# FoX output projection by block products, with GpSimd making the weight sums and two of the seven products beside the last pass of attention

## The chip, the cores and the metric

The kernel runs on one core of a Trainium2 chip. A core has TensorE (PE: matmuls, with its weight loads in a row of their own, PEld), VectorE (DVE), ScalarE (ACT), GpSimd (POOL) and SyncE (SP), which here issues all DMAs. The metric is the time of one execution on the device in microseconds (us), as the median of several runs.

## The reference

Two layers on 1024 tokens of width 1024, float32. Each layer has a token mixer (forgetting attention in layer 0, gated linear attention, GLA, in layer 1) and a SwiGLU part of hidden width 2816, both normed before, modulated by a conditioning vector and added back with a gate. The change touches the last product of the first mixer, `o @ w_out`, a 1024 x 1024 by 1024 x 1024 product whose result is gated and added to `x`.

```python
def forgetting_attention(h, w_in, b_f, w_out):
    ...
    for blk in range(S // Q_BLOCK):
        ...
        p = jax.nn.softmax(logits, axis=-1).astype(v.dtype)
        outs.append(jnp.einsum('bhqk,bkhd->bqhd', p, v[:, :qe]))
    o = jnp.concatenate(outs, axis=1).reshape(B, S, D_MODEL)
    return o @ w_out

def reference(...):
    ...
        x = x + g1[:, None, :] * y
        h = modulate(rms_norm(x, norm2_g[i]), sh2, sc2)
        x = x + g2[:, None, :] * swiglu(h, ffn_w_in[i], ffn_w_out[i])
    return rms_norm(x, final_g)
```

## The kernel before

**Layout.** Activations lie transposed: feature tiles of 128 partitions by 1024 tokens, eight of them, each in two token halves of 512. A product of float32 matrices is made of three matmuls in TensorE's rounded format: each operand is split into a high part (a cast on ScalarE) and a low part (a subtraction on VectorE or GpSimd), and `mm3` (L304) adds high times high, high times low and low times high into one PSUM bank. `split` (L173) does this for activations. `load_w` (L220) does it for weights: a DMA into one of the three raw buffers `wr`, two casts on ScalarE, and the low part in four quarters, three on GpSimd and one on VectorE, into a pair of buffers of the ring `ws`. `Weights` (L290) holds the list of all weight loads in program order and keeps up to `depth` of them issued ahead.

**Order.** All engines run their own instructions in order. The order on each engine is chosen when the program is built, by a scheduler that follows the program order and moves ready work ahead. `weave` (L130) interleaves two generators by their stated costs.

**Attention.** Eight passes of two heads, p = 0 to 7. `attention(p)` (L1356) takes, for each head, four groups of 256 queries in the order 0, 3, 1, 2 (L1344). `scores` makes logits on TensorE, a minimum on VectorE (L1287), the exponential on ScalarE (L1291), a reciprocal on VectorE (L1292) and the scaling on GpSimd (L1293). `outputs` transposes the probabilities on TensorE, splits them and multiplies with v; the result goes to a tile `oT` (L1342). One group's outputs are made behind the next group's scores. After passes 0 to 6 the tile is stored to `oT_d` (L1354); that of pass 7 stays on the chip. In the loop at L1384 each pass is woven with the q, k and v projections of the next one (`qk_proj`, L1246, and `v_half`). Until pass 7 small steps of the conditioning (`ada0`, raw rows also in `wr`) run beside.

**The FoX output projection.** `fox_tail` (L1459) is woven with pass 7 (L1474). It reloads o tiles 0 to 3 from `oT_d`, splits them into `oh`, and `out_chunk` (L1412) multiplies k tiles 0 to 3 with the weights for eight output tiles and two token halves, adding each result with the gate to `xs` on VectorE (L1431). Behind it, in `ffn` (L1494), `last_chunk` (L1436) does k tiles 4 to 7, first token half 0, then token half 1, and sums the squares (`SumSq`, L759) for the norm. The norm of half 0 (L1543, with L1533 and L1541) runs while TensorE does half 1; the feed-forward matmuls begin right behind, `plain_tile` (L1669), with the norm of half 1 inside them. The weights come in by `out_loads` (L882, L1062): four loads for k tiles 0 to 3, and four for k tiles 4 to 7, twice.

**Layer 1** already makes its output projection by block products (`out_blocks`, L2392, and `out_ends`, L2467), with weight sums made ahead on GpSimd (`ow_sums`, L985), and hands them to `ffn` by its argument `blocks`.

Of the kernel before, what the change touches and what calls it, by code (L numbers as in the profile page):

```python
# [9 lines left out]
F32 = mybir.dt.float32  # L10
# [6 lines left out]
P = 128  # L17
# [36 lines left out]
def trunk(ctx, tc, x, c, ada_w, ada_b, norm1_g, norm2_g, ffn_w_in, ffn_w_out,  # L54
# [972 lines left out]

    OW_G = (0, 1, 2)

    def ffn_loads(l):  # L1030

        blk = lambda gr, ab, *after: (op_block, l, gr, ab, *after)
# [24 lines left out]
    for p in range(7):  # L1057
# [200 lines left out]

    oTs = {}

    def scores(u):

# [189 lines left out]


    idle = [s_ for s_ in list(vring.q)[:4] + list(qk_free)[:3]]
    oh = new_h("oh")
    x_slots = idle + [list(otr.q)[-1]]
    xs = [big.tile([P, S], F32, tag=x_slots[k], name=f"x0_{k}") for k in range(8)]

    def fox_tail():  # L1459
        for k in range(4):  # L1460
            reload_h(oT_d, oh, k, "or")

        nc.sync.dma_start(xs[0], xT_d[0])

        def ahead(k):
            if 3 <= k < 6:
                reload_h(oT_d, oh, k + 1, "or")
            if k < 7:
                nc.sync.dma_start(xs[k + 1], xT_d[k + 1])
            yield 0.01  # L1470
# [1078 lines left out]
```

## Time and profile before

| what | value |
|---|---|
| median of 3 runs | 2354.34 us (2350.84 to 2356.11) |
| the profiled execution | 2352.71 us, its span 2351.0 us |
| granted TensorE clock, mean | 0.996 |
| share of the span: PE, DVE, ACT, POOL | 99%, 76%, 48%, 48% |
| DMA moved | 383.38 MB, mean 163 GB/s |

A row of the timeline gives the start, the duration, the engine, the line, the operation, the tiles (written <- read) and the shapes; a bracket gives idle time of the engine ahead of it and what ended it. A row of groups gives the count, the busy time, the mean duration in ns of one, and the idle time ahead. A row of stretches gives the length and then, for each engine, busy time and the count of instructions, at the end the granted clock, the share of the DMA engines and the GB/s. The times of one view are those of one execution. Buffer numbers are left out of names; `fo0470p_b` is the bank for k tiles from 4, output tile 7, of the first run over token half 0.

### The profile page before, as it was taken

To read this page: it belongs to the slowest core of one execution; us is meant where nothing else is said; L and a number is where in the kernel's file an instruction comes from. 1 tells how busy PE (TensorE), PEld (TensorE's weight loads), DVE (VectorE), ACT (ScalarE), POOL (GpSimd) and SP (SyncE) were. 2 spreads that over 40 slices of the span, in tenths; PEclk is the share of its full clock that TensorE was granted. 3 is DMA by queue.
4 is the path that set the end of the run, shared out by engine and by line. 5 is a ranking of instruction groups with operands and counts; after the bars stand their busy time and mean duration, and the time that the engine had idled before them with its cause. 6 is when DMAs were issued, how large, how long until landed. Compare 5 with 4: busy or idle time off the path is not lost. (4 is left out here: it accounts for less than half of the span.)

```text
span 2351.0 us, 35555 instructions
## 1 busy us (share of the span) xinstructions
PE 2327.1 (99%) x12168; PEld 1981.4 (84%) x12168; DVE 1780.7 (76%) x2947; ACT 1121.9 (48%) x2166; POOL 1139.3 (48%) x1005
## 2 busy tenths in 40 slices
PE   8999999999999999999999999999999999999999
PEld 7888888888888888888888898898888888888888
DVE  6578787886688888886787665568787777876887
ACT  6666566665453333344334644345544333345236
POOL 1334444533355656664563431335456666664651
PEclk8999999999999999999999999999999999999999
DMA  8423343332435545458774443455434544458674
GB/s 263 149 85 109 104 122 95 122 126 99 129 101 178 188 157 172 156 180 305 261 255 156 143 127 90 140 179 170 140 111 158 176 149 159 139 189 299 238 262 142
DMA packets 349614, 383.38 MB, mean 163 GB/s; under 512 B 25372, under 2 KB 286648, under 8 KB 349432
## 3 DMA queue, kind: packets, MB, share of 16 engines
q1 hardware_dynamic: 349432, 381.11, 49.3%
q8 instruction: 96, 1.57, 0.3%
q14 instruction: 86, 0.70, 0.1%
HBM read 279.76 MB, written 101.25 MB: 162 GB/s over the span
## 5 line engine op out<-in xcount | busy, mean ns | idle before, releaser
L174 ACT CAST o_s<-xv_s 128x512 fp32r<-128x512 f32 (+1 forms) x392 | 236.4, 610 | 340.2 <-PE p_b L307 257.2
L175 DVE TENSOR_TENSOR o_s<-xv_s,o_s 128x512 fp32r<-128x512 f32 (+1 forms) x392 | 336.5, 863 | 43.7 <-ACT o_s L174 43.0
L307 PE MATMUL p_b<-B,o_s 128*128 128x512 f32 x608 | 236.0, 389 | 0.0
L306 PE MATMUL p_b<-B,o_s 128*128 128x512 f32 x608 | 235.9, 389 | 0.0
L305 PE MATMUL p_b<-B,o_s 128*128 128x512 f32 x608 | 235.4, 390 | 0.0
L1293 POOL TENSOR_SCALAR lp_s<-lp_s,st 128x128 f32<-128x128 f32 (+7 forms) x128 | 96.9, 761 | 247.9 <-DVE st L1292 229.0
L940 POOL TENSOR_TENSOR ex_s<-xv_s,xv_s 128x512 f32<-128x512 f32 (+1 forms) x64 | 94.8, 1481 | 239.8 <-DMA xv_s<-in_ffn_w_in_dram 121.9
L305 PE MATMUL p_b<-T,o_s 128*128 128x512 f32 x480 | 186.8, 389 | 0.0
L306 PE MATMUL p_b<-T,o_s 128*128 128x512 f32 x480 | 186.7, 389 | 0.0
L307 PE MATMUL p_b<-T,o_s 128*128 128x512 f32 x480 | 181.2, 389 | 0.0
L307 PEld LDWEIGHTS p_b<-B,o_s 128*128 128x128 f32 x608 | 114.1, 188 | 23.9
L305 PEld LDWEIGHTS p_b<-B,o_s 128*128 128x128 f32 x608 | 114.1, 188 | 23.7 <-DVE x L1659 0.2
L306 PEld LDWEIGHTS p_b<-B,o_s 128*128 128x128 f32 x608 | 114.1, 188 | 23.5
L1291 ACT ACTIVATE lp_s<-lp_s,st 128x128 f32<-128x128 f32 (+7 forms) x128 | 99.3, 776 | 57.9 <-DVE st L1287 56.5
L942 POOL TENSOR_TENSOR xv_s<-ex_s,xv_s 128x512 f32<-128x512 f32 (+1 forms) x64 | 93.8, 1466 | 60.6 <-DVE o_s L175 57.7
L1659 DVE TENSOR_TENSOR ex_s<-ex_s,p_b 128x512 f32<-128x512 f32 x140 | 94.2, 681 | 38.0 <-PE p_b L307 37.8
L174 ACT CAST pt_s<-t_b 128x512 fp32r<-128x512 f32 (+1 forms) x160 | 79.7, 547 | 73.5 <-PE t_b L1313 72.9
L952 POOL TENSOR_TENSOR xv_s<-xv_s,xv_s 128x512 f32<-128x512 f32 x48 | 65.5, 1364 | 92.3 <-issue 50.4
L175 DVE TENSOR_TENSOR pt_s<-t_b,pt_s 128x512 fp32r<-128x512 f32 (+1 forms) x160 | 96.2, 630 | 15.9 <-ACT pt_s L174 15.4
L246 POOL TENSOR_TENSOR w_l_s<-w__s,w_h_s 128x256 fp32r<-128x256 f32 x90 | 69.4, 800 | 77.1 <-ACT w_h_s L242 59.2
L307 PEld LDWEIGHTS p_b<-T,o_s 128*128 128x128 f32 x480 | 90.1, 188 | 18.7
L306 PEld LDWEIGHTS p_b<-T,o_s 128*128 128x128 f32 x480 | 90.1, 188 | 18.7
(1527 smaller groups left out, 7409.5 us busy)
## 6 DMA issues: line engine op xcount, KB each, us to landing
xv_s<-in_ffn_w_in_dram SPq DMA_DIRECT2D x176, 256.0 KB, 3.3
hid_B<-x SPq DMA_DIRECT2D x66, 512.0 KB, 2.8
ad_s<-in_ada_w_dram SPq DMA_DIRECT2D x384, 64.0 KB, 2.4
hid_T<-x SPq DMA_DIRECT2D x44, 512.0 KB, 2.9
xv_s<-in_ffn_w_out_dram SPq DMA_DIRECT2D x88, 256.0 KB, 3.5
ada_s<-in_ada_w_dram SPq DMA_DIRECT2D x96, 128.0 KB, 2.8
T2o<-hid_T SPq DMA_DIRECT2D x22, 512.0 KB, 7.5
T1o<-hid_T SPq DMA_DIRECT2D x22, 512.0 KB, 6.2
```

What stands on the lines that cost most here:

```text
L174: nc.scalar.copy(hi, src)
L175: nc.vector.tensor_sub(lo, src, hi.bitcast(F32))
L246: (nc.gpsimd if i < 3 else nc.vector).tensor_sub(lo[:, cs], rw[:, cs], hi[:, cs].bitcast(F32))
L305: nc.tensor.matmul(ps, ah, bh, start=start, stop=False, skip_group_check=chain)
L306: nc.tensor.matmul(ps, ah, bl, start=False, stop=False, skip_group_check=chain)
L307: nc.tensor.matmul(ps, al, bh, start=False, stop=stop, skip_group_check=chain)
L940: nc.gpsimd.tensor_add(s1, a21, a22)
L942: nc.gpsimd.tensor_sub(a11, s1, a11)
L952: nc.gpsimd.tensor_sub(r[A12], r[A12], r[A11])
L1291: nc.scalar.activation(lp, lp, AF.Exp, bias=mcur, scale=-1.0, accum_out=st[:, qi, 2:3])
L1293: nc.gpsimd.tensor_scalar(lp, lp, st[:, qi, 3:4], 1.0, op0=ALU.mult, op1=ALU.mult)
L1659: nc.vector.tensor_add(d, d if src is None else dest(G, src), ps)
```

## The change

The projection is made by the seven products of the Winograd form of Strassen's algorithm, one level deep: the 8 output tiles are taken as four pairs g, the k tiles and the tokens are halved. With a = o tiles 0 to 3 and c = o tiles 4 to 7, and the index for the token half, the activation blocks are B11 = a1, T1 = a0 - a1, T2 = c0 - T1, T3 = c0 - a0, B22 = c0, B21 = c1, T4 = c1 - T2. On the weight side A11, A12 and A22 are blocks of the weights, and four sums (called 5, 6, 3 and 7) are made by `fox_sums`: eight steps in passes 2 to 5 load a part of the weights, make the sums with four GpSimd operations each and store them in DRAM (`fw_d`). `fox_loads` reads 14 weight loads of the old size: blocks or sums.

Beside pass 7, `fox_tail` now makes B11 and T1 (two pairs g at a time, two banks), and the splits of T2 and B22 for the three o tiles that are stored. Behind it come `fox_blocks` (T2, B22, T3) and, as the end with the norm beside it, `fox_ends` (B21 and T4, output tile by output tile), both called from `ffn` by its argument `blocks`. The differences of activations are on GpSimd but for one. a and c are reloaded for T3, B21 and T4 into slots that attention used. Results are still added to `xs` on VectorE, 40 times in place of 32.

```diff
+    fw_d = {(nm_, g): tc.dram_tile([HALF, P], F32, name=f"fw{nm_}{g}") for nm_ in (5, 6, 7, 3) for g in range(4)}
+    def fox_src(g, ab):
+        return fox_w_out[0][psl(4 * ab[1], 4), psl(2 * g + ab[0])]
+    def fox_sums():
+        for g in range(4):
+            for s_ in (0, 2):
+                t = wr([P, 2, 2, 2 * P], F32, f"fw{g}{s_}")
+                for h in range(2):
+                    nc.sync.dma_start(t[:, h], fox_w_out[0][psl(4 * h + s_, 2), psl(2 * g, 2)]
+                                      .rearrange("(k p) m -> p k m", p=P))
+                (a11, a21), (a12, a22) = ((t[:, h, :, 0:P], t[:, h, :, P:2 * P]) for h in range(2))
+                nc.gpsimd.tensor_add(a22, a21, a22)
+                nc.gpsimd.tensor_sub(a21, a11, a21)
+                nc.gpsimd.tensor_sub(a11, a22, a11)
+                nc.gpsimd.tensor_sub(a12, a12, a11)
+                for nm_, a in ((5, a22), (7, a21), (6, a11), (3, a12)):
+                    nc.sync.dma_start(fw_d[(nm_, g)].rearrange("(k p) m -> p k m", p=P)[:, s_:s_ + 2], a)
+                yield
+    def fox_loads():
+        two = lambda a, b, nm_: (load_w, (a, b), nm_)
+        r = [two(fox_src(g, A11), fw_d[(5, g)], f"fa{g}") for g in range(4)]
+        r += [two(fw_d[(nm_, g)], fw_d[(nm_, g + 1)], f"f{nm_}{g}") for nm_ in (6, 3, 7) for g in (0, 2)]
+        return r + [two(fox_src(g, A12), fox_src(g, A22), f"fe{g}") for g in range(4)]
...
-    loads += out_loads(fox_w_out[0], 0, 4) + 2 * out_loads(fox_w_out[0], 4, 4)
+    loads += fox_loads()
...
+        if 1 < p < 6:
+            next(fw_sums)
...
+    fw_sums = fox_sums()
...
+    F_SL = {"B11": 0, "T3": 0, "T1": 4, "B21": 4, "T2": 8, "T4": 8, "B22": 12}
+    fa3 = big.tile([P, S], F32, tag=acc_sl[0], name="fa3")
+    def fb_split(nm_, k, y, lo_=nc.vector):
+        t = fb[nm_][k] = big.tile([P, 2, HALF], FR, tag=H_SL[F_SL[nm_] + k], name=f"fb{nm_}{k}")
+        nc.scalar.copy(t[:, 0], y)
+        lo_.tensor_sub(t[:, 1], y, t[:, 0].bitcast(F32))
+    def fox_raw(k, t=None):
+        t = wr([P, S], F32, f"or{k}") if t is None else t
+        nc.sync.dma_start(t, oT_d[k])
+        return t
+    def fox_prod(ps, w, c, t, ks, start):
+        for k in ks:
+            mm3(ps, w.hi[:, k, psl(c)], w.lo[:, k, psl(c)], t[k][:, 0], t[k][:, 1], start and k == ks[0],
+                k == ks[-1], True)
+            yield 0.65
+    def fox_add(m, hf, ps):
+        nc.vector.scalar_tensor_tensor(xs[m][:, hsl(hf)], ps, mcol(0, 2, m), xs[m][:, hsl(hf)],
+                                       op0=ALU.mult, op1=ALU.add)
     def fox_tail():
-        for k in range(4):
-            reload_h(oT_d, oh, k, "or")
...
-        yield from out_chunk(0, 4, oh, xs, 0, 2, "fo", (0, 1), before=ahead)
-    weave(attention(7), 27.0, fox_tail(), 36.0, LAGS)
-    split(oh[7].hi, oh[7].lo, oTs[7])
+        for k in ALL:
+            a = fox_raw(k, fa3 if k == 3 else None)
+            fb_split("B11", k, a[:, h1_])
+            if k < 3:
+                nc.gpsimd.tensor_sub(a[:, h0_], a[:, h0_], a[:, h1_])
+                fb_split("T1", k, a[:, h0_])
+            else:
+                nc.gpsimd.tensor_sub(a[:, h1_], a[:, h0_], a[:, h1_])
+                fb_split("T1", k, a[:, h1_])
+        for m in (0, 1):
+            nc.sync.dma_start(xs[m], xT_d[m])
+        feed.depth = 2
+        for g in (0, 2):
+            ws_, ps_ = [], []
+            for i in range(2):
+                ws_.append(feed.next())
+                ps_.append(pj([P, HALF], F32, f"fo{g + i}p"))
+                yield from fox_prod(ps_[i], ws_[i], 0, fb["B11"], ALL, True)
+                for m in (2 * (g + i), 2 * (g + i) + 1):
+                    fox_add(m, 1, ps_[i])
...
+            for i in range(2):
+                k = g + i
+                if k < 3:
+                    c, a = fox_raw(4 + k), fox_raw(k)
+                    nc.gpsimd.tensor_sub(a[:, h1_], a[:, h1_], a[:, h0_])
+                    nc.gpsimd.tensor_add(a[:, h1_], c[:, h0_], a[:, h1_])
+                    fb_split("T2", k, a[:, h1_])
+                    fb_split("B22", k, c[:, h0_])
+                yield from fox_prod(ps_[i], ws_[i], 1, fb["T1"], ALL, False)
+                for m in (2 * (g + i), 2 * (g + i) + 1):
+                    fox_add(m, 0, ps_[i])
+    weave(attention(7), 27.0, fox_tail(), 21.0, LAGS)
+    def fox_blocks(views):
+        feed.depth = 3
+        c3, pa, w6 = oTs[7], [bank(i, [P, HALF], f"fp{i}") for i in (0, 1, 6, 7)], []
+        for g in ALL:
+            if g % 2 == 0:
+                w6.append(feed.next())
+            run(fox_prod(pa[g], w6[-1], g % 2, fb["T2"], range(3), True))
+        nc.vector.tensor_sub(fa3[:, h1_], c3[:, h0_], fa3[:, h1_])
+        fb_split("T2", 3, fa3[:, h1_])
+        fb_split("B22", 3, c3[:, h0_])
+        for g in ALL:
+            run(fox_prod(pa[g], w6[g // 2], g % 2, fb["T2"], (3,), False))
+            fox_add(2 * g, 0, pa[g])
+        ac = []
+        for k in range(3):
+            a, c = (big.tile([P, S], F32, tag=slots["b"][2 * k + i], name=f"fr{k}{i}") for i in range(2))
+            fox_raw(k, a)
+            fox_raw(4 + k, c)
+            ac.append((a, c))
+        ac.append((fa3, c3))
+        for a, c in ac:
+            nc.gpsimd.tensor_sub(a[:, h0_], c[:, h0_], a[:, h0_])
+        for k, (a, c) in enumerate(ac):
+            fb_split("T3", k, a[:, h0_])
+        sv = views()
+        sq = SumSq(sv, 0, LATE1)
+        for g in ALL:
+            pb = bank(2 + g, [P, HALF], f"fq{g}")
...
+            run(fox_prod(pb, w, g % 2, fb["B22"], ALL, True))
+            fox_add(2 * g, 0, pb)
+            sq(g, xs[2 * g][:, h0_])
+        for k, (a, c) in enumerate(ac):
+            if k < 3:
+                nc.gpsimd.tensor_add(a[:, h1_], a[:, h0_], a[:, h1_])
+            fb_split("B21", k, c[:, h1_])
+            nc.gpsimd.tensor_sub(c[:, h1_], c[:, h1_], a[:, h1_])
+        for g in ALL:
...
+            run(fox_prod(pa[g], w, g % 2, fb["T3"], ALL, False))
+            fox_add(2 * g + 1, 0, pa[g])
+            sq(4 + g, xs[2 * g + 1][:, h0_])
+            fox_add(2 * g + 1, 1, pa[g])
+            fb_split("T4", g, ac[g][1][:, h1_])
+        return sq, sv
+    def fox_ends(sv, behind):
+        sq = SumSq(sv, 1, LATE1, False)
+        for m in range(8):
...
+            ps = bank((2, 3, 4, 5, 0, 1, 4, 5)[m], [P, HALF], f"fe{m}")
...
+                run(fox_prod(ps, w, m % 2, fb["T4" if m % 2 else "B21"], ALL, True))
+            fox_add(m, 1, ps)
+            sq(m, xs[m][:, h1_])
+        return sq
...
-    ffn(0, oh, xs, slots, "fo", lambda: mid(0, 1), norm_mixer)
+    ffn(0, None, xs, slots, "fo", lambda: mid(0, 1), norm_mixer, None, (fox_blocks, fox_ends))
```

More of the change, by code (lines that the diff above doesn't have):

```diff
@@ L1474, in trunk @@
-    weave(attention(7), 27.0, fox_tail(), 36.0, LAGS)
-    split(oh[7].hi, oh[7].lo, oTs[7])
+    h0_, h1_ = hsl(0), hsl(1)
+    ALL = range(4)
+    F_SL = {"B11": 0, "T3": 0, "T1": 4, "B21": 4, "T2": 8, "T4": 8, "B22": 12}
+    fb = {nm_: [None] * 4 for nm_ in F_SL}
+    fa3 = big.tile([P, S], F32, tag=acc_sl[0], name="fa3")
[3 more added lines that the diff above has]
+        lo_.tensor_sub(t[:, 1], y, t[:, 0].bitcast(F32))
@@ new lines, in trunk @@
+    weave(attention(7), 27.0, fox_tail(), 21.0, LAGS)
[27 more added lines that the diff above has]
+            pb = bank(2 + g, [P, HALF], f"fq{g}")
+            if g % 2 == 0:
+                w = feed.next()
+            run(fox_prod(pb, w, g % 2, fb["B22"], ALL, True))
[7 more added lines that the diff above has]
+        for g in ALL:
+            if g % 2 == 0:
+                w = feed.next()
+            run(fox_prod(pa[g], w, g % 2, fb["T3"], ALL, False))
[4 more added lines that the diff above has]
+        return sq, sv
@@ new lines, in fox_ends @@
+    def fox_ends(sv, behind):
+        sq = SumSq(sv, 1, LATE1, False)
+        for m in range(8):
+            if m % 2 == 0:
+                w = feed.next()
+            ps = bank((2, 3, 4, 5, 0, 1, 4, 5)[m], [P, HALF], f"fe{m}")
+            with ExitStack() as es:
+                for m_, ins in behind:
+                    if m >= m_:
+                        es.enter_context(tc.issue_after(ins))
+                run(fox_prod(ps, w, m % 2, fb["T4" if m % 2 else "B21"], ALL, True))
+            fox_add(m, 1, ps)
+            sq(m, xs[m][:, h1_])
+        return sq
```

12 lines of the change are left out of this document (4 added, 8 removed).

## Prediction

> **What bounds the kernel now.** I read the page first, its span and first part, then the table of stretches (windows) around the place of the change, then single rows of the timeline.
>
> ```profile
> span 2351.0 us, 35555 instructions
> ## 1 busy us (share of the span) xinstructions
> PE 2327.1 (99%) x12168; PEld 1981.4 (84%) x12168; DVE 1780.7 (76%) x2947; ACT 1121.9 (48%) x2166; POOL 1139.3 (48%) x1005
> ```
>
> PE is busy 99% of the span. A busy PE is not yet a PE at its peak, since a 512-column matmul is drawn 0.39 us long and a gap can hide in that, so the spacing of starts decides. These are the last matmuls of the projection and the first of the feed-forward part:
>
> ```profile
> 639.75 0.39 PE L305 MATMUL fo1471p_b<-ohh,wo_768h_s 128*128 128x512 f32 x1
> ...
> 642.24 0.39 PE L307 MATMUL fo1471p_b<-ohh,wo_768l_s 128*128 128x512 f32 x1
> 642.47 0.39 PE L305 MATMUL p_b<-B,o_s 128*128 128x512 f32 x1
> ```
>
> Twelve starts in 2.72 us: one matmul costs 0.2267 us, and the projection hands over without a gap. Now the stretches: passes 2 to 5 of attention (where the weight sums will go), pass 6, pass 7, the rest of the projection, a busy piece of the feed-forward part, and the last 54 us of the GLA output projection, which already works by block products.
>
> ```profile
> core 0: us, PE busy (x) PEld busy (x) DVE busy (x) ACT busy (x) POOL busy (x), PEclk, DMA share, GB/s
> 190.00:442.00 252.00, 249.63 (x1658) 221.52 (x1658) 198.86 (x496) 154.27 (x333) 126.42 (x184) 1.00 0.36 111
> 472.60:531.20 58.60, 56.41 (x340) 47.27 (x339) 47.10 (x118) 40.03 (x82) 19.50 (x28) 1.00 0.39 128
> 531.20:604.00 72.80, 72.71 (x425) 62.05 (x424) 45.73 (x117) 35.51 (x79) 24.40 (x32) 1.00 0.24 85
> 604.00:642.40 38.40, 38.40 (x178) 31.76 (x177) 29.61 (x43) 21.48 (x36) 16.91 (x17) 1.00 0.51 165
> 660.00:700.00 40.00, 40.00 (x178) 33.14 (x177) 39.78 (x58) 21.54 (x37) 17.21 (x7) 1.00 0.28 86
> 1643.00:1697.00 54.00, 54.00 (x247) 44.95 (x246) 41.33 (x57) 27.49 (x46) 27.96 (x20) 1.00 0.40 127
> ```
>
> The clock is 1.00 throughout. Pass 7 loses 0.09 us of PE time in 72.8, since the projection's first 192 matmuls fill the waits of attention; pass 6, with half as many fillers (96 matmuls of the last q and k projections), loses 2.19 us in 58.6. The rest of the projection loses nothing. So every matmul taken out here is worth its 0.2267 us as long as the other engines keep up, and VectorE, at 63% and 77% in the third and fourth row, is the one to watch.
>
> **The change, part by part.** *Matmuls.* Before: 8 column tiles, 2 token halves, 8 k tiles, 3 matmuls each, 384. After: 7 products of 4 column pairs, 4 k tiles, 3 matmuls, 336. Gone: 48 x 0.2267 = **-10.9 us**. Beside pass 7 stand 96 instead of 192, behind it 240 instead of 192. So pass 7 shrinks by up to 96 x 0.2267 = 21.8 us, to 51, and the part behind it grows by 10.9, to 54.4 us.
>
> *Thinner cover of pass 7.* Its fillers then have the density of pass 6. At that row's idle share (2.19 / 58.6) a stretch of 51 us loses 1.9 us. VectorE's work in it hardly shrinks: where three oh splits fall away, six half-width splits of T2 and B22 come, and the 16 adds stay:
>
> ```profile
> L175 DVE TENSOR_TENSOR ohl<-or_s,ohh x7: 1204/1226/1627, 503.9 to 550.5; 128x1024 fp32r<-128x1024 f32 x7
> ```
>
> So about 46 of 51 us, 90%, with score reductions queued behind splits. I take **+3 us**, one more than the row, as gaps also hide in the drawn length. Bounds: 0 (nothing lost, as in pass 7 now) and 6, three times the row's share.
>
> *Weight sums.* Eight steps, each two loads of 256 KB, four GpSimd operations on 256 elements and four stores of 128 KB, in passes 2 to 5. The nearest row:
>
> ```profile
> L468 POOL TENSOR_TENSOR acc_s<-acc_s 128x256 f32<-128x256 f32 x26 | 19.2, 740 | 1.2
> ```
>
> 32 x 0.74 = 23.7 us on a GpSimd that is half idle there (126.4 of 252). What hides it is PE's own work, 249.6 of 252. Queued behind it on GpSimd are the softmax scalings (L1293), on SyncE the weight and ada loads, when a store waits for GpSimd; each step also takes one turn of the three raw buffers (wr), which weights and ada rows share:
>
> ```profile
> engine line waited for: us in total, times, longest us
> DVE acc_s L505 <- DMA ada_s<-in_ada_w_dram: 8.4, 5, 2.1
> ```
>
> PE lost 2.37 us there with 126 us of GpSimd work; in proportion 23.7 us more cost **+0.5 us**, my value. Bounds 0 and 5: eight such waits of 2.1 us, of which PE feels at most 2.37 / 8.4.
>
> *Behind pass 7.* VectorE gets 28 splits of 512 columns for 8 of 1024, 40 adds for 32, and a quarter of 14 weight loads for 12; ScalarE the matching casts (it is half idle). GpSimd gets 11 differences of 512 columns here (and 10 beside pass 7). Some of those run one after the other with VectorE, as these two answers (VectorE, then GpSimd) show:
>
> ```profile
> 1645.64 1.78 DVE L175 TENSOR_TENSOR goB<-gs_s,goB 128x512 fp32r<-128x512 f32 x1
> ...
> 1648.66 0.68 DVE L175 TENSOR_TENSOR goT<-og_s,goT 128x512 fp32r<-128x512 f32 x1
> ```
>
> ```profile
> 1645.12 1.74 POOL L1025 TENSOR_TENSOR ow_s<-xv_s,ow_s 128x512 fp32r<-128x512 f32 x1
> 1647.49 1.30 POOL L2450 TENSOR_TENSOR gs_s<-gs_s,og_s 128x512 f32<-128x512 f32 x1 [0.63 <-DVE goB L175]
> ```
>
> The same split takes 0.68 us alone and 1.78 when a GpSimd operation has begun 0.52 us ahead of it; it ends 0.56 us after that one. GpSimd takes 1.30 alone. So I add up the two engines' SBUF work as if they shared one door. Durations of the other kinds:
>
> ```profile
> 538.06 0.41 DVE L246 TENSOR_TENSOR wo_768l_s<-wo_s,wo_768h_s 128x256 fp32r<-128x256 f32 x1
> ...
> 589.21 0.48 DVE L1287 CUSTOM_DVE_ANT_0 lp_s<-s_b,cum_s,st 128x256 f32<-128x256 f32 x1
> ...
> 603.54 0.42 DVE L1342 TENSOR_TENSOR oT_s<-o_b,ot 64x256 f32<-64x256 f32 x1 [0.86 <-ACT ot L1341]
> ...
> 621.71 0.73 DVE L1431 SCALAR_TENSOR_TENSOR x<-fo0470p_b,modc,x 128x512 f32<-128x512 f32 x1
> ...
> 631.91 5.35 DVE L1533 SCALAR_TENSOR_TENSOR ya_s<-x,amul,rb_b 128x512 f32<-128x512 f32 x8
> ...
> 638.38 0.75 DVE L1541 SCALAR_TENSOR_TENSOR B<-ya_s,modc,B 128x512 fp32r<-128x512 f32 x1
> ```
>
> ```profile
> 557.57 2.32 POOL L246 TENSOR_TENSOR wo_0l_s<-wo_s,wo_0h_s 128x256 fp32r<-128x256 f32 x3 [1.61 <-ACT wo_0h_s L242]
> ...
> 591.59 0.90 POOL L1293 TENSOR_SCALAR lp_s<-lp_s,st 128x768 f32<-128x768 f32 x1 [4.78 <-DVE st L1292]
> 595.12 2.31 POOL L246 TENSOR_TENSOR wo_512l_s<-wo_s,wo_512h_s 128x256 fp32r<-128x256 f32 x3 [2.63 <-ACT wo_512h_s L242]
> 601.66 2.31 POOL L246 TENSOR_TENSOR wo_256l_s<-wo_s,wo_256h_s 128x256 fp32r<-128x256 f32 x3 [4.23 <-ACT wo_256h_s L242]
> 612.03 2.14 POOL L246 TENSOR_TENSOR wo_768l_s<-wo_s,wo_768h_s 128x256 fp32r<-128x256 f32 x3 [8.06 <-ACT wo_768h_s L242]
> ...
> 629.47 1.02 POOL L715 TENSOR_TENSOR rs<-rs,mhalf 128x4 f32<-128x4 f32 x1
> ```
>
> GpSimd: 11 x 1.30 + 10 loads x 2.32 + 4 sums of squares x 1.30 + the root, 1.0 = 43.7 us. VectorE with both inputs in SBUF: 14 splits and one difference x 0.68 + 10 x 0.41 + 6 sums of squares x 0.68 + five norm splits x 0.75 + four feed-forward weights x 0.68 = 24.9 us. Together 68.6 us for a part of 54.4: 14.2 too many if nothing is done ahead. But the slots of T3's raw tiles are free when the last scores are reduced (589.7), 14 us before the last attention output (603.5), and in the 20 us from 592 to 612 GpSimd works under 6. The 9 differences of the six reloaded tiles (11.7 us), three T3 splits (2.0) and the first two loads (5.5) fit there: 19.2 us against 14.2. It fits, with little to spare. On VectorE alone the 24 adds (24 x 0.73 = 17.5) and eight norm products (5.35) on top make about 48 us of 54.4, between the fourth row of the table (77%) and the GLA row (77%) and the 99% of 660 to 700, where PE still loses nothing. The narrow place is the end: before, the last add of token half 0 started at 621.7, the first norm split at 638.4, and PE took it up at 642.5, 4.1 us later; now four T4 splits (2.7 us) and the weights' share for the end products (1.6) stand ahead of the norm in VectorE's queue. I take **+2 us**. Bounds: 0, as the GLA row has it (PE 54.0 of 54), and 14.2, if nothing gets ahead.
>
> The Trainium skill, page "SBUF — State Buffer", section "SBUF: two separate sides", speaks against the change here: it says that GpSimd and a VectorE operation with two SBUF inputs hold a shared pair of ports by turns, for a whole instruction, and the later one blocks. The trace agrees (1.78 for 0.68). By a plain overlap of the two engines this part would cost 0, by that rule anything up to the 14.2 above.
>
> *Transfers.* Behind pass 7 come six reloads (3 MB) and two weight loads more (1 MB): the row's 165 GB/s x 38.4 us = 6.3 MB become 10.5 MB in 54.4 us, 193 GB/s. The page's slices show more than that elsewhere:
>
> ```profile
> GB/s 263 149 85 109 104 122 95 122 126 99 129 101 178 188 157 172 156 180 305 261 255 156 143 127 90 140 179 170 140 111 158 176 149 159 139 189 299 238 262 142
> ```
>
> So nothing is added; the bound is +1 us.
>
> *Sum*: -10.9 + 3 + 0.5 + 2 = **-5.4 us**. The profiled execution took 2352.7 us, 1.7 around its span of 2351.0, so it would take 2347.3. The median of the three runs, 2354.3, lies 1.6 higher; from there I forecast **2348.9 us**. About 0.2%, 4.7 us, is what a measurement of this kernel can tell from no change.
>
> **The rivals.** *All of it is kept.* Nothing but the sums costs anything: -10.4, 2343.9 us. For it: GLA, same products, PE 54.0 of 54. Against it: there no softmax chain runs beside them.
>
> *The last pass is bound by VectorE.* Pass 7 loses the 6 us of its bound, and the 4.3 us of splits that stand ahead of the norm delay the feed-forward part in full: -10.9 + 6 + 0.5 + 4.3 = -0.1, 2354.2 us. For it: 90% of VectorE in 51 us, and pass 6 losing 2.19 at 80%. Against it: the weights and the casts run ahead on other engines. This is also the case in which the change does what it says and nothing comes of it.
>
> *Slower: GpSimd and VectorE by turns.* T3's reloads land after pass 7, the 11 differences stand behind weight splits in GpSimd's queue, VectorE's splits wait for them, and PE waits for T3 and T4: the 14.2 us come in full, -10.9 + 3 + 0.5 + 14.2 = +6.8, 2361.1 us. It decides from the point where more than 7.4 us of the 14.2 fail to get ahead (10.9 - 3 - 0.5). For it: 68.6 us for 54.4, and the reloads are issued late in the program. Against it: GpSimd's idle 14 us ahead, and SyncE free to load there. The shared ports of the page named above are this mechanism.
>
> **How the numbers follow.** Forecast (-2.5 to -8) 0.46; all kept 0.16; bound by VectorE 0.24; slower by turns 0.14. Of the forecast two thirds (0.31) lie beyond 4.7 us: faster 0.16 + 0.31 = 0.47. Slower by over 4.7 us: most of the last case, 0.13, and 0.02 of the third: 0.15. The rest, 0.38, is within 0.2%. The range goes from 2342.5 (all kept, less the spread of the runs) to 2358.5, half-way into the slower case; some 0.1 lies above and 0.08 below. The forecast's own range is 2346 to 2352.
>
> **What would show it.** Right: 336 matmuls of the projection at 0.227; pass 7 shorter by 18 to 20 us with 2 to 4 us of PE idle in it; GpSimd's T3 differences before the last attention output; the first feed-forward matmul within 2 us of the last one of the projection; passes 2 to 5 as long as before within 1 us. Wrong: T3 or T4 matmuls waiting for a split behind GpSimd (slower case); score reductions late behind T1, T2 and B22 splits (third case); waits for ada or weight loads in passes 2 to 5, or a gap where the second token half of the feed-forward part begins.

## The result, and the profile after

The changed kernel took 2379.22 us (median of four runs, 2376.09 to 2380.26), the kernel before 2354.82 beside it. The ratio is 1.0107, with a 95% interval from 1.0095 to 1.0119. It is slower by about 25 us; forecast were 5 us less, and the range up to 2358.5 did not hold the time.

The head of the page of the changed kernel:

```profile
span 2377.6 us, 35758 instructions
## 1 busy us (share of the span) xinstructions
PE 2331.4 (98%) x12120; PEld 1983.5 (83%) x12120; DVE 1795.3 (76%) x2978; ACT 1132.1 (48%) x2190; POOL 1200.3 (50%) x1064
```

There are 48 matmuls fewer, as the change says, and the span is 26.6 us longer. To see where, I cut both traces at the last output matmul of each pass and at the first matmul of the feed-forward part. These are the stretches of the kernel before: passes 1 to 4 (this is where the weight sums are made; the prediction called these passes 2 to 5), pass 5, pass 6, pass 7, and the rest up to the feed-forward part.

```profile
core 0: us, PE busy (x) PEld busy (x) DVE busy (x) ACT busy (x) POOL busy (x), PEclk, DMA share, GB/s
172.80:423.50 250.70, 248.33 (x1650) 220.14 (x1649) 197.10 (x499) 152.11 (x328) 123.33 (x179) 1.00 0.36 109
423.50:484.70 61.20, 59.96 (x393) 52.61 (x391) 48.01 (x123) 37.07 (x79) 28.98 (x42) 1.00 0.38 124
484.70:540.90 56.20, 54.48 (x331) 45.93 (x331) 46.09 (x113) 39.36 (x82) 20.73 (x29) 1.00 0.42 143
540.90:602.80 61.90, 61.90 (x361) 52.89 (x360) 38.06 (x95) 29.17 (x62) 18.11 (x24) 1.00 0.19 66
602.80:642.50 39.70, 39.70 (x185) 32.84 (x184) 30.12 (x44) 21.86 (x37) 18.07 (x19) 1.00 0.50 160
```

And the same five in the changed kernel:

```profile
core 0: us, PE busy (x) PEld busy (x) DVE busy (x) ACT busy (x) POOL busy (x), PEclk, DMA share, GB/s
175.10:434.50 259.40, 252.05 (x1647) 222.55 (x1646) 196.32 (x496) 152.40 (x328) 141.76 (x207) 0.99 0.44 133
434.50:495.70 61.20, 59.59 (x393) 52.57 (x392) 48.48 (x125) 37.04 (x79) 31.29 (x44) 1.00 0.40 123
495.70:554.50 58.80, 53.28 (x317) 44.70 (x315) 45.35 (x119) 39.54 (x87) 27.83 (x32) 0.97 0.46 150
554.50:618.90 64.40, 54.68 (x304) 45.24 (x302) 52.32 (x107) 35.20 (x76) 39.97 (x40) 0.92 0.41 131
618.90:668.90 50.00, 45.31 (x210) 37.47 (x209) 40.98 (x63) 25.66 (x45) 22.97 (x24) 0.99 0.48 155
```

The projection's matmuls stand 58, 161 and 165 in the last three stretches before, and 42, 104 and 190 after (counted in the two traces; the scheduler also drew 50 matmuls of T2 and B22 forward into pass 7). At 0.2267 us each, pass 6 should have become 3.6 us shorter and the rest after pass 7 5.7 us longer. So the stretches lost:

| stretch | length | matmuls moved | lost |
|---|---|---|---|
| up to the end of pass 0 | +2.3 | 0 | 2.3 |
| passes 1 to 4 | +8.7 | 0 | 8.7 |
| pass 5 | 0.0 | 0 | 0.0 |
| pass 6 | +2.6 | -3.6 | 6.2 |
| pass 7 | +2.5 | -12.9 | 15.4 |
| rest of the projection | +10.3 | +5.7 | 4.6 |
| feed-forward part to the end | +0.2 | 0 | 0.2 |

The column adds up to 37.4, and 37.4 - 10.9 = 26.5 us, which is the difference of the spans (26.6) but for rounding. Pass 0 is the same work in all kernels here but two, and took between 172.7 and 176.5 us in their fourteen traces, so its 2.3 us are scatter. The 0.2 us of the last row is a balance of two losses: the changed kernel loses 2.9 us behind the handover to a slow clock (last section), and the kernel before has a pause and a slow clock of its own in that part (2.21 us at 1500.5 and a granted clock of 0.50 in the 3.4 us from 1500.8). Three places are left.

**The end of pass 7.** VectorE there, then TensorE, from the timeline of the changed kernel:

```profile
603.60 1.75 DVE L1498 TENSOR_TENSOR fbT<-fr,fbT 128x512 fp32r<-128x512 f32 x1 [2.98 <-POOL fr L1575]
605.27 1.75 DVE L1498 TENSOR_TENSOR fbB<-fr,fbB 128x512 fp32r<-128x512 f32 x1
606.95 1.74 DVE L1498 TENSOR_TENSOR fbT<-fr,fbT 128x512 fp32r<-128x512 f32 x1
608.72 0.42 DVE L1374 TENSOR_TENSOR oT_s<-o_b,ot 64x256 f32<-64x256 f32 x1
```

```profile
603.89 1.39 PE L1345 MATMUL t_b<-ident,lp_s 128*128 128x128 f32 x11
609.29 0.36 PE L1359 MATMUL o_b<-pt_s,v_s 128*128 128x256 f32 x1 [4.01 <-DVE oT_s L1374]
612.51 1.22 PE L1359 MATMUL o_b<-pt_s,v_s 128*128 128x256 f32 x4 [2.87 <-DVE pt_s L175]
```

Three splits of T3 and B21, raw tiles `fr`, stand on VectorE ahead of an attention output (L1374); the first of them waits 2.98 us for GpSimd. The first T3 product starts at 625.0 and the first B21 product at 640.4, 20 us later and more, but TensorE waits 4.01 us for that output and then 2.87 us for splits of probabilities. The windows of 4 us show what follows:

```profile
604.00:608.00 4.00, 1.28 (x12) 1.04 (x10) 4.00 (x3) 2.89 (x7) 4.00 (x3) 1.00 0.02 4
608.00:612.00 4.00, 0.36 (x1) 0.19 (x1) 3.94 (x6) 0.73 (x2) 4.00 (x5) 0.74 0.00 0
612.00:616.00 4.00, 3.49 (x10) 3.00 (x11) 4.00 (x5) 1.75 (x3) 3.92 (x3) 0.50 0.44 131
616.00:620.00 4.00, 4.00 (x21) 3.35 (x20) 2.00 (x4) 0.74 (x2) 0.00 (x0) 0.91 0.00 0
```

VectorE and GpSimd are both busy all the time while TensorE stands, and when its work comes back, the granted clock is 0.50 for four microseconds: the pause is paid partly twice.

**The handover.** TensorE, and then VectorE, at the first feed-forward matmul:

```profile
663.81 0.39 PE L307 MATMUL fe<-fbT,fe3l_s 128*128 128x512 f32 x1
668.89 0.77 PE L305 MATMUL p_b<-B,o_s 128*128 128x512 f32 x1 [4.69 <-DVE x L1512]
```

```profile
660.17 0.75 DVE L1682 SCALAR_TENSOR_TENSOR B<-ya_s,modc,B 128x512 fp32r<-128x512 f32 x1
...
667.99 1.41 DVE L1512 SCALAR_TENSOR_TENSOR x<-fe,modc,x 128x512 f32<-128x512 f32 x2
```

The norm's first split (L1682) begins 3.6 us before the projection's last matmul. What the first feed-forward matmul waits for is the add of an end product (L1512): a PSUM bank, not data (the bank order of e4, below, closes the gap).

**Passes 1 to 4.** In pass 1 the row of an ada load comes late, the chain of its steps (L505) bunches, and two score matmuls wait for VectorE. Before the change the same chain stood four steps long here, after it six. (Long series are not new in themselves: of the 66 steps in these passes, 22 stand in series of four or more before the change and 31 after it, and the longest has seven in both.)

```profile
218.07 2.05 DVE L505 SCALAR_TENSOR_TENSOR acc_s<-ada_s,c,acc_s 128x256 f32<-128x256 f32 x4 [1.47 <-DMA ada_s<-in_ada_w_dram]
```

```profile
216.06 0.48 DVE L505 SCALAR_TENSOR_TENSOR acc_s<-ada_s,c,acc_s 128x256 f32<-128x256 f32 x1 [3.64 <-DMA ada_s<-in_ada_w_dram]
...
222.72 3.07 DVE L505 SCALAR_TENSOR_TENSOR acc_s<-ada_s,c,acc_s 128x256 f32<-128x256 f32 x6
```

```profile
229.72 0.33 PE L1313 MATMUL s_b<-KA,QA 128*128 128x128 f32 x1 [1.50 <-DVE st L1319]
```

### The profile page after: what moved, and what is told of

Read it like the earlier page. It is cut to its first block, busy times and chain, and to the rows that moved or that the text cites. A ratio compares the mean times of both kernels' runs of the same rounds, so it can differ in the third digit from the quotient of the medians.

```text
span 2377.6 us, 35758 instructions
## 1 busy us (share of the span) xinstructions
PE 2331.4 (98%) x12120; PEld 1983.5 (83%) x12120; DVE 1795.3 (76%) x2978; ACT 1132.1 (48%) x2190; POOL 1200.3 (50%) x1064
## 5 line engine op out<-in xcount | busy, mean ns | idle before, releaser
L174 ACT CAST o_s<-xv_s 128x512 fp32r<-128x512 f32 (+1 forms) x392 | 236.4, 610 | 341.4 <-PE p_b L307 256.0
L1359 PE MATMUL o_b<-pt_s,v_s 128*128 128x256 f32 x512 | 98.5, 299 | 11.1 <-DVE oT_s L1374 4.7
## 6 DMA issues: line engine op xcount, KB each, us to landing
xv_s<-in_ffn_w_in_dram SPq DMA_DIRECT2D x176, 256.0 KB, 3.2
xv_s<-in_ffn_w_out_dram SPq DMA_DIRECT2D x88, 256.0 KB, 4.0
```

The costliest lines, as they stand in the source:

```text
L174: nc.scalar.copy(hi, src)
L1359: nc.tensor.matmul(ops, lv, pts[b][:, hl, 2 * jj:2 * jj + 2, :], start=j == 0 and hl == 0, stop=False)
```

## The experiments

Where an expectation speaks of lost matmul spacing, this is, over all matmuls of a stretch, the distance to the next start less the median distance for that shape in the whole execution. Before the change it is 9.8 us in passes 1 to 4, 6.1 in passes 6 and 7 and 0.4 in the rest of the projection; after it 18.9, 27.7 and 5.0. Ratios are to the kernel before on the same chip.

### The weight sums alone, and the changed kernel without them

e1 adds `fox_sums` and its call to the kernel before. e2 takes the call out of the changed kernel and loads plain blocks of the weights where that reads sums, so its products do not make the projection:

```diff
-        r = [two(fox_src(g, A11), fw_d[(5, g)], f"fa{g}") for g in range(4)]
-        r += [two(fw_d[(nm_, g)], fw_d[(nm_, g + 1)], f"f{nm_}{g}") for nm_ in (6, 3, 7) for g in (0, 2)]
+        r = [two(fox_src(g, A11), fox_src(g, A22), f"fa{g}") for g in range(4)]
+        r += [two(fox_src(g, A12), fox_src(g + 1, A11), f"f{nm_}{g}") for nm_ in (6, 3, 7) for g in (0, 2)]
...
-        if 1 < p < 6:
-            next(fw_sums)
```

> The kernel before with the eight weight-sum steps added and nothing else; the sums are stored and not used. Theory 1 (the sums cost what passes 1 to 4 lost in the trace of after: 9 us of PE time, by ada rows that land late behind the sums' stores on SyncE): +7 to +11 us on before, 2362 to 2366 us, with waits of VectorE's chain step for ada rows of over 3 us. Rival (the prediction's 0.5 us; what passes 1 to 4 lost comes from the changed order of the whole program): -1 to +2 us, 2353 to 2357 us.

> The changed kernel without the weight sums: the weight loads read plain blocks of the weights where they read sums, same bytes, so the seven products are taken with wrong weights. Theory 1: passes 1 to 4 take as long as before within 2 us, and the kernel 7 to 11 us less than the changed one: 2368 to 2372 us. Rival (order of the program): within 2 us of the changed kernel, 2377 to 2381 us.

e1 took 2357.06 us, ratio 1.0019 (1.0010 to 1.0027): +4.2 us, between the two. e2 took 2371.09, ratio 1.0075 (1.0061 to 1.0089): 7.5 us below the changed kernel, as theory 1 has it. Passes 1 to 4 lasted 258.3 us in e1 and 251.8 in e2, against 250.7 before and 259.4 after. So the loss of passes 1 to 4 is the sums' and not that of another order of the program; e1 got some of it back later (pass 6 was 1.5 us shorter than before). The sums cost 4 to 8 us, of which e1's 4.2 stand without any other part of the change.

### Which part of the sums

e7 leaves out the stores, e8 the GpSimd operations, e12 all but the turn of the raw buffer (each on top of e1). This is a step of e12 beside one of e1; its one-column memset is what takes the turn:

```diff
                 t = wr([P, 2, 2, 2 * P], F32, f"fw{g}{s_}")
-                for h in range(2):
-                    nc.sync.dma_start(t[:, h], fox_w_out[0][psl(4 * h + s_, 2), psl(2 * g, 2)]
-                                      .rearrange("(k p) m -> p k m", p=P))
...
-                nc.gpsimd.tensor_add(a22, a21, a22)
...
+                nc.gpsimd.memset(t[:, 0, 0, 0:1], 0.0)
```

> The kernel before with the weight sums added as in e1, but without their four stores per step (the sums are not used). If the loss of passes 1 and 3 (4.6 and 2.3 us of matmul spacing in the trace of e1) comes from SyncE, which waits in its stores for GpSimd with the ada rows queued behind: both under 1 us. If it comes from GpSimd's operations or the loads: unchanged, 4.6 and 2.3.

> The kernel before with the weight sums' loads and stores added as in e1, but without the 32 GpSimd operations (raw weights are stored and not used). If the loss comes from GpSimd sharing a way to SBUF with VectorE, or from GpSimd's own queue: under 1 us in passes 1 and 3. If it comes from the turns of the raw buffers and SyncE's order of loads and stores: 3 to 7 us remain.

> The kernel before, where each of the eight steps of the weight sums only takes its turn of the three raw buffers and writes one column there on GpSimd: no loads, no other operations, no stores. If the turn is what costs (the next weight or ada row waits for the buffer): 3 to 8 us of matmul spacing more than before in passes 1 to 4, as in e7 (passes 1 and 3: 3.6 and 3.3 us) and e8. If it is the transfers and operations together: under 1.5 us.

Each was run once (2354.99, 2363.73 and 2357.78 us; the kernel before took 2351.63 beside the first two and 2353.22 beside the third). Passes 1 to 4 lasted 257.2 us without stores, 264.7 without operations, and 256.6 with the turns alone, against 250.7: no part has to be there for the loss but the turn. In lost spacing over that of the kernel before, e7 has 3.6 us in pass 1 and 3.3 in pass 3, and e12 4.9 in the four passes together. SyncE's wait in the stores, which I had read out of the trace of after, is therefore not the cause. What is left in all of them is the turn, and with it the order that the scheduler draws around the eight steps; no run parts these two. In e12, where the sums transfer nothing, the timeline still shows six ada steps in a row, right ahead of a score reduction:

```profile
221.36 3.53 DVE L505 SCALAR_TENSOR_TENSOR acc_s<-ada_s,c,acc_s 128x256 f32<-128x256 f32 x6
224.80 0.55 DVE L1304 CUSTOM_DVE_ANT_0 lp_s<-s_b,cum_s 128x384 f32<-128x384 f32 x1
```

My reading is that a turn of the three raw buffers given to the sums puts off the ada row that would have had it, its steps pile up, and in VectorE's fixed order they stand ahead of attention. That fits these rows; it is not shown for the whole of the loss.

Passes 1 to 4 lasted between 254.9 and 263.3 us in nine traces of kernels with the same sums at the same places. Most of that scatter is the clock. The shortest, e6, and the longest, e3, have almost the same matmuls:

```profile
175.00:429.90 254.90, 248.82 (x1646) 219.78 (x1646) 194.54 (x496) 152.29 (x328) 142.12 (x207) 1.00 0.44 135
173.10:436.40 263.30, 256.21 (x1647) 226.14 (x1646) 195.67 (x496) 152.52 (x328) 142.34 (x207) 0.97 0.42 131
```

In these passes the granted clock is 0.50 for 0 us in e6 and for 17.1 in e3. Less half of the time at 0.50, which is an estimate of what the slow clock cost, the nine traces lie between 253.8 and 256.0 us, the kernel before at 250.7 and e2 at 250.1, e7 at 253.8, e8 at 256.2 and e12 at 256.6. So the work of the sums in these places costs 3 to 6 us, the turns alone no less than the whole, and the rest is slow clock behind the pauses. Each of these figures is of one profiled execution.

### The sums at another place

e10 has the bank order of e4 (below), and the steps behind the v projections:

```diff
             v_split(g, tp, ps)
+            if g in (1, 2):
+                next(fw_sums)
...
-        if 1 < p < 6:
-            next(fw_sums)
```

> The changed kernel with the bank order of e4, and the eight weight-sum steps made one by one behind the v projections of passes 0 to 3, away from the places where ada rows are asked for (before: in pairs beside them, passes 1 to 4). If the sums cost because their turns of the three raw buffers bunch the ada rows: 4 to 7 us below e4, +12 to +15 us on the kernel before, and passes 1 to 4 lose under 3 us more than before in the trace. If a step costs about the same wherever it stands: within 2 us of e4, +17 to +20 us.

2378.06 us, ratio 1.0113 (1.0098 to 1.0128): worse than either expectation, 8 us above e4 by the ratios. Passes 1 to 4 lasted 264.6 us. The steps now take turns beside the v weights, and in pass 2, where the changed kernel lost nothing, TensorE has a pause of 1.68 us (at 301.65) behind a late scaling of GpSimd. The rows of GpSimd show what made it late:

```profile
297.54 0.74 POOL L1044 TENSOR_TENSOR fw_s<-fw_s 128x256 f32<-128x256 f32 x1 [2.13 <-DMA fw_s<-in_fox_w_out_dram]
...
300.69 1.71 POOL L1325 TENSOR_SCALAR lp_s<-lp_s,st 128x768 f32<-128x768 f32 x3
```

The first operation of a sum step waits 2.13 us for its load, all four stand ahead of the scaling, and the scaling starts 2.0 us after VectorE has made its reciprocals (298.65). So here the operations of the sums cost time, in GpSimd's order, which e8 and e12 could not show. Series of ada steps do not explain e10: 18 of the 66 stand in series of four or more, fewer than before the change, and yet it takes longer than any kernel with the steps at the first place once the slow clock is left out (262.9 us). My picture, sums beside ada rows, was too narrow: what a step costs goes by what stands behind it at its place.

### The order of the banks

```diff
-            pj.q.rotate(2)
+            pj.q.rotate(2 if l else -2)
```

> The changed kernel with the six PSUM banks taken in another order by the feed-forward part, so that its first product takes the bank of the first end product and not of the seventh. Theory 3 (the first feed-forward matmul waits 4.7 us for the add of that seventh product, which stands behind eight norm splits on VectorE, and a clock of 0.50 to 0.65 follows for 8 us): 5 to 9 us less, 2370 to 2374 us, and no gap over 1 us at the handover. Rival (the norm's own splits are late, with VectorE at its limit in the tail, as the prediction's tail term had it): -2 to +1 us, 2377 to 2380 us, with the gap moved to the splits.

2371.54 us, ratio 1.0079 (1.0065 to 1.0093), 6.6 us below the changed kernel, as theory 3 says. The rest of the projection lasts 45.1 us in place of 50.0, with the same 190 matmuls, and the handover is closed:

```profile
662.18 0.39 PE L307 MATMUL fe<-fbT,fe3l_s 128*128 128x512 f32 x1
662.40 0.61 PE L305 MATMUL p_b<-B,o_s 128*128 128x512 f32 x2
```

The ring gave the first feed-forward product bank 4. In layer 1 that is the bank of the third of eight end products, here that of the seventh, whose add stood behind the norm. Behind the handover 24 matmuls start in 5.44 us, as in the kernel before, where the changed kernel needed 8.31: no slow clock followed.

### T3 and B21 held behind attention

```diff
-            fb_split("T3", k, a[:, h0_])
+            with tc.issue_after(ends[0]), tc.issue_after(ends[1]):
+                fb_split("T3", k, a[:, h0_])
...
-            fb_split("B21", k, c[:, h1_])
+            with tc.issue_after(ends[0]), tc.issue_after(ends[1]):
+                fb_split("B21", k, c[:, h1_])
```

`ends` are the last copy (L1373) and the last output add (L1374) of pass 7. e11 holds T2 and B22 of the last tile too, on top of e10, and puts the norm's matmuls two products later.

> The changed kernel with the casts and splits of T3 and B21 held, on ScalarE and VectorE, behind the last attention output of pass 7. Theory 2 (three of these splits, 1.75 us each beside GpSimd, stood on VectorE ahead of the last outputs and cost PE the pauses of 4.0 and 2.9 us at 605 to 613 us, and then a clock of 0.5 to 0.9): 5 to 10 us less, 2369 to 2374 us. Rival (they are only moved, and PE waits for T3 and B22's partner splits behind the pass instead; the tail is short of VectorE time): -1 to +3 us, 2378 to 2382 us.

> e10, with the casts and splits of T3 and B21 and also the last parts of T2 and B22 held behind the last attention output, and the norm's first matmuls two products later in TensorE's queue. If e3 lost in the tail only by the bank order and the norm's place in TensorE's queue: pass 7 loses 11 us or less (17 before the hold), the tail under 3 us, and the time is 3 to 9 us below e10. If the tail has no room for the held work on VectorE (what is taken out of pass 7 is paid behind it): -2 to +5 us on e10, with waits for T3's and T4's splits behind the pass.

e3: 2381.57 us, ratio 1.0123 (1.0109 to 1.0137). e11: 2381.31, 1.0125 (1.0110 to 1.0140), 2.8 us above e10. Both times the rival was nearer: the loss is only moved, and by the ratios e3 lies even 3.8 us above the changed kernel. These are e11's stretches, pass 7 and the rest:

```profile
560.60:614.50 53.90, 49.73 (x298) 41.70 (x298) 38.75 (x95) 28.92 (x65) 32.16 (x37) 1.00 0.45 147
614.50:666.10 51.60, 48.63 (x214) 39.28 (x214) 44.29 (x64) 29.77 (x54) 30.23 (x28) 0.97 0.45 143
```

Pass 7 lasted 64.6 us in e10 and 53.9 here (1.1 of it by five matmuls fewer). But the rest went from 45.2 to 51.6 and the feed-forward part, with the norm of half 1, from 1705.3 to 1711.6; 6.1 of these 6.3 us fall in the time of its first 150 matmul starts (37.45 us in place of 31.35). VectorE is busy 38.8 us in pass 7, where the changed kernel had 52.3, and 44.3 of 51.6 us behind it, 86%; there the splits stand ahead of adds and norm. In e3, TensorE waited 5.35 us for the sum of squares.

### The work for T2 and B22, and the cover

e5 brings tiles of the shape of T2 and B22 for three k tiles by transfers, with no differences, casts or splits; e6 makes the matmuls beside pass 7 twice; e9 does both. None of the three makes the projection.

```diff
-                    c, a = fox_raw(4 + k), fox_raw(k)
-                    nc.gpsimd.tensor_sub(a[:, h1_], a[:, h1_], a[:, h0_])
-                    nc.gpsimd.tensor_add(a[:, h1_], c[:, h0_], a[:, h1_])
-                    fb_split("T2", k, a[:, h1_])
-                    fb_split("B22", k, c[:, h0_])
+                    c, a = 4 + k, k
+                    fb_dma("T2", k, a)
+                    fb_dma("B22", k, c)
```

```diff
                 yield from fox_prod(ps_[i], ws_[i], 0, fb["B11"], ALL, True)
+                yield from fox_prod(ps_[i], ws_[i], 0, fb["B11"], ALL, False)
...
                 yield from fox_prod(ps_[i], ws_[i], 1, fb["T1"], ALL, False)
+                yield from fox_prod(ps_[i], ws_[i], 1, fb["T1"], ALL, False)
...
-    weave(attention(7), 27.0, fox_tail(), 21.0, LAGS)
+    weave(attention(7), 27.0, fox_tail(), 42.0, LAGS)
```

> The changed kernel with T2 and B22 for the three stored o tiles brought by one transfer each in place of their GpSimd differences, ScalarE casts and VectorE splits, so that they hold plain o tiles (the values are wrong, the products stand as before). Theory 4 (passes 6 and 7 lose their time because this work stands ahead of the score reductions, the softmax scalings and the casts of the probabilities on three engines): 6 to 12 us less than the changed kernel, 2366 to 2372 us on a chip where the kernel before takes 2353. Rival (the cover is thin: 96 matmuls beside pass 7 are too few, and the chain of attention itself sets the time): within 3 us of the changed kernel, 2375 to 2381 us.

> The changed kernel with each of the 96 matmuls beside pass 7 made twice (the sums are doubled, so the output is wrong), 192 as before, and nothing else beside that pass changed. They are 96 x 0.2267 = 21.8 us of TensorE. Thin cover: half or more of them vanish in pauses that stand there anyway: +4 to +12 us on the changed kernel, 2382 to 2390 us. Theory 4 (other engines' queues): the pauses stay, +17 to +24 us, 2395 to 2402 us.

> e5 and e6 together: T2 and B22 for three o tiles by transfers, and the 96 matmuls beside pass 7 made twice (values wrong in both ways). In the traces, passes 6 and 7 lost 27.7 us of matmul spacing in the changed kernel, 18.8 in e5 and 16.9 in e6, against 6.1 before. If work in the other queues and thin cover are two causes that add up: 8 us or less are left, and the time is 7 to 11 us below e6, +26 to +30 us on the kernel before. If they are one loss seen twice (either remedy hides the same pauses): 14 us or more are left, within 4 us of e6, +33 to +38 us on before.

e5: 2371.36 us, ratio 1.0082 (1.0057 to 1.0106), about 6 us below the changed kernel, at the lower end of theory 4; its four runs lie 13.6 us apart, so that its interval reaches into that of the changed kernel and its traced stretches say more than its time. e6: 2389.08, 1.0158 (1.0141 to 1.0174): of 21.8 us of added matmuls only 12 are seen. e9: 2386.89, 1.0146 (1.0129 to 1.0163). The stretches of passes 6 and 7, first e5, then e9:

```profile
492.40:547.60 55.20, 51.42 (x316) 43.09 (x315) 42.78 (x114) 37.60 (x83) 22.40 (x28) 1.00 0.53 180
547.60:606.70 59.10, 52.36 (x304) 43.70 (x302) 50.26 (x105) 34.16 (x74) 37.69 (x38) 0.94 0.37 125
```

```profile
494.80:556.10 61.30, 58.35 (x344) 49.57 (x343) 43.27 (x114) 36.55 (x82) 22.44 (x28) 0.97 0.48 162
556.10:628.20 72.10, 66.73 (x370) 56.41 (x370) 50.30 (x108) 36.21 (x75) 37.28 (x38) 0.95 0.31 103
```

With the same matmuls as the changed kernel (58.8 + 64.4 = 123.2 us), e5 needs 114.3, 8.9 less; the four traces in which passes 6 and 7 have the same work (the changed kernel, e2, e4, e10) lie between 123.1 and 127.6. e9, with 96 matmuls more, needs 133.4: 19.1 us more than e5, so that once the work for T2 and B22 is gone, nearly all added matmuls cost their time. The lost spacing of the two passes is 27.7 us in the changed kernel, 18.8 in e5, 17.0 in e6 and 16.3 in e9: what one remedy takes away, the other does not take away again. So it is in the main one loss seen from two sides, as e9's second expectation said: splits and differences stand ahead of the steps of attention, and TensorE feels it where it has nothing else to do. Neither remedy touches the last pauses; in e9, TensorE still waits 2.50 and 2.87 us at 618 to 621 us for the same rows as above.

### The differences of T3 and T4

On top of e4, e13 leaves out the 11 GpSimd differences behind pass 7, and e14 makes them on VectorE:

```diff
-            nc.gpsimd.tensor_sub(a[:, h0_], c[:, h0_], a[:, h0_])
+            nc.vector.tensor_sub(a[:, h0_], c[:, h0_], a[:, h0_])
```

> e4 without the 11 GpSimd differences of T3 and T4 (the tiles are split as they come, so the values are wrong; casts, splits, loads and products stay). If pass 7 and the tail suffer from these differences (splits that wait for them, and VectorE and GpSimd by turns): pass 7 loses 10 us or less (17.5 in e4) and the time is 6 to 12 us below e4, +7 to +13 us on the kernel before. If the splits' place ahead of the last attention outputs is enough: within 4 us of e4, +15 to +20 us.

> e4 with the same 11 differences on VectorE in place of GpSimd. If the two engines' turns are what makes them dear (the same operation took 0.68 us on VectorE alone, 1.30 on GpSimd, 1.75 for a split beside it): 2 to 8 us below e4, +11 to +17 us on the kernel before. If VectorE's own time is the limit in pass 7 (52.3 us busy of 64.4) and the tail: 1 to 8 us above e4, +19 to +27 us.

e13: 2370.46 us, ratio 1.0072 (1.0055 to 1.0090). e14: 2372.13, 1.0080 (1.0063 to 1.0096). Beside e4's 1.0079 neither makes a difference that can be told. VectorE at the end of pass 7 in e13:

```profile
605.84 1.29 DVE L1498 TENSOR_TENSOR fbT<-fr,fbT 128x512 fp32r<-128x512 f32 x2 [2.23 <-ACT fbT L1497]
607.27 0.69 DVE L1498 TENSOR_TENSOR fbB<-fr,fbB 128x512 fp32r<-128x512 f32 x1
607.88 1.82 DVE L1498 TENSOR_TENSOR fbT<-fr,fbT 128x512 fp32r<-128x512 f32 x2
609.62 0.94 DVE L246 TENSOR_TENSOR f70l_s<-f_s,f70h_s 128x256 fp32r<-128x256 f32 x1
610.59 0.42 DVE L1374 TENSOR_TENSOR oT_s<-o_b,ot 64x256 f32<-64x256 f32 x1
```

The splits take 0.69 us, not 1.75, and the first waits for a cast in place of a difference; five of them and a weight's share still stand ahead of the same output, and TensorE's pause there is 2.89 us (4.01 in the changed kernel). e14 fell between its two expectations: the work is dearer on GpSimd by the row, and moving it changes nothing that can be told.

## Why the prediction was wrong, step by step

- **Matmuls, -10.9: right.** 336 of them, at a median spacing of 0.227 us.
- **Thinner cover of pass 7, +3 (0 to 6): the step that failed.** Passes 6 and 7 lost 21.6 us. The bound was three times the idle share of pass 6 before, and that row says nothing of three things. VectorE's load in pass 7 was not the 46 us that I reckoned but 52.3, with eight splits of T3, B21 and T4 among it (11.0 us), drawn in there although their products come some 20 us later and more. In an order fixed ahead, a split that stands in the wrong place, or waits for its operand, stops the whole chain of scores, scalings and outputs (the rows above and e5 show this; e13 shows that GpSimd's differences need not be there for it; e3 and e11 show that behind the pass there is no room for it either). And the longer pauses are followed by a lower clock. I had looked at sums of busy time where the question was who stands ahead of whom.
- **Weight sums, +0.5 (0 to 5): 4 to 8 us.** I costed the GpSimd operations, which PE's work hides, and named the turn of the raw buffer beside them as a cost of eight waits. The turn is what costs at these places (e12, one run), in pass 1 by bunched ada steps on VectorE as far as the rows show; how the rest comes about stays open. In another place the GpSimd operations stand ahead of the scalings (e10), as the prediction feared. In proportion to GpSimd's work was the wrong scale.
- **The tail, +2 (0 to 14.2): 4.6 us and 2.9 of slow clock behind it, by another cause.** The bank order makes all of it (e4: 0.1 us of lost spacing in the same stretch, 5.0 in the changed kernel). With the other order the tail costs nothing, as the GLA row said. The changed kernel's code shows the ring and the bank list of `fox_ends`; I followed the engines' queues and not who frees the bank.
- **Transfers, 0: right.** 155 GB/s in the rest of the projection, and from pass 6 on to its end TensorE waits for no transfer; GpSimd does, at the longest 5.5 us for the first reloaded tile of T3.
- **The clock, no term.** The prediction read 1.00 throughout and left it there. In the changed kernel's trace the granted clock is 0.50 for 27.3 us between the end of pass 0 and 2340 us, in that of the kernel before for 3.4. Half of TensorE's busy time in these stretches, an estimate of what they cost, is 11.8 us against 1.7, so that about 10 of the 26.6 us are paid behind the pauses and not in them; they are contained in the losses above.
- **The rivals.** Slower than before is what came, but not by turns of GpSimd and VectorE: VectorE did wait 2.98 us for one of T3's differences, yet e13 and e14 lie within 2 us of e4 by the ratios. The shared ports, which the Trainium skill describes on the page "SBUF — State Buffer", section "SBUF: two separate sides", are seen again (1.75 us for a split beside GpSimd, 0.69 without), but they do not decide. The rival "the last pass is bound by VectorE" named the right place and engine, priced by the same bound of 6 us.

What stays open: whether some order of VectorE's work serves both attention's end and the products behind it. Of the versions run, none is as fast as the kernel before; the best of those that make the projection by the seven products is e4, at 1.0079. Open too is how the turns of the sums reach TensorE outside pass 1.

## What to carry to other kernels

Extra work beside a latency-bound chain isn't priced by busy shares: ask of each moved operation what stands behind it in its engine's order, and bound a cover that is halved by what the chain loses without cover, not by a multiple of what it loses with it. When the end of a part is rewritten, follow its PSUM banks (and its ring buffers) into the part behind it. A step that uses a shared ring can cost its turn, however small its work (eight turns cost 4 to 6 us here).

## What was not expected of the hardware

The longer pauses of TensorE are paid a second time by the clock here. After the 4.69 us at the handover, the granted clock was 0.50 and then 0.65 in two windows of 4 us.

```profile
664.00:668.00 4.00, 0.20 (x1) 0.00 (x0) 4.00 (x8) 0.63 (x1) 0.00 (x0) 0.99 0.45 160
668.00:672.00 4.00, 3.11 (x7) 2.48 (x8) 3.96 (x6) 2.52 (x3) 2.44 (x2) 0.50 0.96 343
672.00:676.00 4.00, 4.00 (x13) 3.20 (x12) 1.37 (x1) 0.00 (x0) 0.82 (x1) 0.65 0.08 28
676.00:680.00 4.00, 4.00 (x20) 3.29 (x19) 0.00 (x0) 0.60 (x1) 0.00 (x0) 1.00 0.00 0
```

By the rows, (1 - 0.50) x 3.1 + (1 - 0.65) x 4 = 3.0 us are lost in these two windows on top of the pause itself. The starts agree: 24 matmuls from the first one of the feed-forward part take 8.31 us here and 5.44 in the kernel before and in e4, 2.87 us less.

In the trace, the 0.65 is a mean: from 668.0 to 674.8 the granted clock is 0.50, and then 1.00 again. All traces here show it so, in stretches of 3.4, 6.8 or 10.2 us from pass 1 on. Pauses much shorter than these can bring one: in the changed kernel a pause of 1.46 us that ended at 571.2 was followed by 3.4 us at 0.50 from 572.4; TensorE had been busy for 55% of the 3.4 us before that. Others of that length brought none, as one of 1.99 us at 412.3 in the kernel before.
